# First attention's heads, the state space taps' layout and the phase corrections, reordered in one tuned kernel

## The chip, the cores and the metric

The kernel runs on one core of a Trainium2 chip. The metric is the device time of one execution in microseconds (us); the median of three runs is 1253.97 us (1253.89 to 1257.54). A core has five engines with a queue of their own each: PE (TensorE; its weight loads are shown as PEld), DVE (VectorE), ACT (ScalarE), POOL (GpSimd) and SP (SyncE), which issues most DMAs; ACT and POOL can issue DMAs too. An engine works its queue in order, and waits where an instruction's input isn't there or its output buffer isn't free.

## The reference

Two blocks and a feed-forward part over 512 tokens of 1024 columns, in float32. The change lies in the first block, which joins a state space mixer and sparse attention:

```python
ssm_u, ssm_z, q, k, v, attn_z, q_idx, k_idx, w_idx = jnp.split(h @ w_in[l], ...)
# s5_mixer: 32 groups of 16 channels, 64 complex states each
bu = jnp.einsum('gpc,bsgc->bsgp', b_bar, ug)
_, states = lax.associative_scan(_ssm_combine, (a_seq, bu), axis=1)
y = jnp.einsum('gcp,bsgp->bsgc', c_mat, states).real + d_skip * uf
z = jax.nn.gelu(y); z = z * jax.nn.sigmoid(z @ w_glu + b_glu)
# dsa_mixer: 8 heads of 64; an indexer of 8 heads picks 128 keys per query
q, k = rms_norm(q, q_gain), rms_norm(k, k_gain)
score = jnp.einsum('bqh,bqhs->bqs', wib, jax.nn.relu(rel))
_, sel = lax.top_k(score, topk)
logits = einsum(q, k[sel]) * scale + rel_bias[bucket(dist)]
```

The second block (a pooling mixer and attention over compressed, selected and window keys) and the feed-forward part are computed as before in both kernels.

## The kernel before, in words

**Order of work.** The program text is a set of generators. `weave(main, fill)` takes a step of the main stream, which asks for some time, and then steps of the filling stream (the projections, in 128x128 products) until that time is used. For PE and SP the order of the text is the order of the queue. For ACT, DVE and POOL a scheduler orders the instructions when the kernel is built, by readiness and by the memory that a step needs. Memory comes from a ring of 49 pages of 128x512 (`pg`, `pages`), and from named pools: the pool "ssm" (`self.sp`) holds the state space tiles, and its `ssmp.__exit__` releases that memory, which the pool "att1" (`self.att`) then takes. So what is written into "att1" waits for the last reader of the state space tiles.

**Products.** A product with a weight is made of three (L153 to L155): each weight chunk `wraw` is split into `whi` (a cast on ACT, L145) and `wlo` (a subtraction on DVE, L146). `proj` makes the queries and keys: a chain of 24 products into a PSUM buffer, then on ACT the copy `qk` (L658) and the square `sq` (L660), then a sum on DVE (L661).

**Index scores and mask.** `index_scores` makes, for three blocks of 256, 384 and 512 columns and 8 heads, a score in one of two PSUM buffers `ps_s` (L941, L942), a `relu` of it into a page on ACT (L944) and a weighted sum on DVE (L948). `top_mask` then runs 16 rounds of a maximum (L964) and a replacement (L965) on each block on DVE.

**State space part.** `ssm_tables` doubles a table of phases, n = 1, 2, 4 to 32, on POOL, and corrects the length of the last phase ahead of each doubling (L1204 to L1210). `ssm_taps` makes `We` and the taps `KK`; `ssm_scan` copies `E` out of PSUM on ACT (L1277), rotates it on POOL (L1281 to L1286), scans on DVE (L1288), rotates back (L1289 to L1294), and ends with `ssm_back` (the tiles `F`, L1228 to L1233) and the tile `TO`: a memset on POOL (L1298) and eight DMAs on ACT's queue (L1300), each a shifted part of `KK`. `bias_flip` transposes the attention's biases (L930) and copies them (`BT`, L931). `ssm_out` then makes for each group two products with a slice of `TO` as weights and four with `F` (L1314, L1318):

```python
nc.tensor.matmul(o[b], lhsT=self.TO[:, :, :, 2 * a + b], rhs=self.U(2 * a + b), start=True, stop=False)
```

A weight element there stands 32 elements behind the one before it. The result goes out on a DMA and comes back as `zi`; a gelu makes `zg` (L1330).

**First attention.** `norms` makes the reciprocal norms `rs`; then "ssm" is released. `attend` runs the heads: `early` of a head multiplies queries and keys by their norms on POOL (`qn` L716, `kn` L720; `qn` for a pair of heads), `prepare` transposes `kn` on PE (L734), splits it into the key stack (L148, L149) and makes the masks `bm` on POOL (L744, L745), and `prepare2` transposes `qn` (L727) and makes the query stacks (L888, L889). The steps of a head are the scores (L341, L342), the row maximum (L343, on DVE), the exponential (L345, ACT), the scaling by `rsum` (L350) and the transposes and products (L369, L383). DVE also works off products for a gate (`wadag`, L898).

Of the kernel before, what the change touches and what calls it, by code (L numbers as in the profile page):

```python
# [12 lines left out]
OP = mybir.AluOpType  # L13
# [48 lines left out]
def layout(inputs):  # L62
# [20 lines left out]
    skip = np.zeros((128, 16, 32), f)  # L83
    skip[112 + np.arange(16), np.arange(16)] = a["d_skip"][0].reshape(32, 16).T
# [20 lines left out]
class Kern:  # L105
# [342 lines left out]
    def block1(self):  # L448
# [238 lines left out]
        z = self.pages("zg", 4)  # L687
# [7 lines left out]
        ssmp.__exit__(None, None, None)  # L695
        attp = self.tc.tile_pool(name="att1", bufs=1)
        self.att = self.grp = attp.__enter__()
        self.qbufs = 4
# [10 lines left out]
        def head(h):  # L709
            hp = h // 2  # L710

            def early():
                if h % 2 == 0:
                    qns[h] = self.att.tile([128, 4, 128], F32, name="qn", tag="qn", bufs=1)
# [3 lines left out]
                kns[h] = self.att.tile([128, 4, 2, 64], F32, name="kn", tag="kn", bufs=1)  # L718
# [4 lines left out]
            def prepare2():  # L723
                if h % 2 == 0:
# [3 lines left out]
                    for hh in range(2):  # L728
                        qsts[h + hh] = self.q_stack(pq, hh, gq[:, 0:1])

            def prepare():
# [3 lines left out]
                kst = [self.att.tile([128, S], F32R, name="kst" + x, tag="kst" + x, bufs=2) for x in "hl"]  # L735
                self.split(pk, kst[0], kst[1], scale=gq[:, 1:2])
                bm = []
                for i in range(4):
                    w = (i + 1) * 128
                    b = self.att.tile([128, w], F32, name=f"bm{i}", tag=f"bm{i}", bufs=1)  # L740
# [56 lines left out]
        self.weave(self.attend([head(h) for h in range(8)], more=1.4), fill)  # L797
# [75 lines left out]
    def q_stack(self, pq, hh, gain):  # L873
        st = self.grp.tile([128, S], F32R, name="qst", tag="qst", bufs=self.qbufs)
        self.stack(st, pq, hh, gain)
        return st
# [200 lines left out]
    def ssm_loads(self):  # L1077
# [4 lines left out]
        self.skip = w[2].rearrange("p (c g) -> p c g", c=16)  # L1082
# [17 lines left out]
    def ssm_tables(self):  # L1100
# [101 lines left out]
        while n < 64:  # L1202

            g = [v[:, :, n - 1] for v in self.turn]  # L1204
            PTT(out=t1, in0=g[0], in1=g[0], op=OP.mult)
            PTT(out=t2, in0=g[1], in1=g[1], op=OP.mult)
            PTT(out=t1, in0=t1, in1=t2, op=OP.add)
            nc.gpsimd.tensor_scalar(t1, t1, -0.5, 1.5, op0=OP.mult, op1=OP.add)
            for v in g:
                PTT(out=v, in0=v, in1=t1, op=OP.mult)  # L1210
# [25 lines left out]
    def ssm_taps(self):  # L1236
# [16 lines left out]
        KK = self.pg("KK").rearrange("p (c g) -> p c g", c=16)  # L1253
        TT(out=KK, in0=kk.rearrange("p (g c) -> p c g", c=16), in1=self.skip, op=OP.add)
        self.KK = KK

    def ssm_scan(self):
# [41 lines left out]
        for r in range(8):  # L1299
            nc.scalar.dma_start(self.TO[0:128 - r * 16, 7 - r], self.KK[r * 16:128])  # L1300

# [558 lines left out]
```

## Time and profile before

| | before |
|---|---|
| median of 3 runs | 1253.97 us (1253.89 to 1257.54) |
| the profiled execution | 1254.35 us |
| its span in the trace | 1252.6 us |
| mean granted clock of PE | 0.974 |
| busy: PE, DVE, ACT, POOL | 92%, 65%, 44%, 37% |

Times of the trace count from the start of the span. A busy time is the time in which an engine has an instruction under way; "idle before" is the time that an engine stood still ahead of an instruction, and the name behind it is the work that ended that wait. Products overlap, so a product's own duration is longer than its share of the time; the distance from one start to the next, its pace, is what counts.

### The profile page before, as it was taken

What the parts mean: (1) busy time and instruction counts of PE and PEld (TensorE: products, weight loads), DVE (VectorE), ACT (ScalarE), POOL (GpSimd) and SP (SyncE); (2) the same over time, 40 slices, a digit from 0 to 9 for tenths busy, and PEclk for the clock granted to TensorE, in tenths of its full rate; (3) what the DMA queues carried; (4) which work ended last, traced back from release to release, by engine and by line L of the source; (5) the groups of instructions that cost most, each with busy time, mean ns of one, the idle gap of its engine ahead of it and who ended that gap; (6) DMA issues with size and microseconds to landing.
All of it is one profiled execution on the core that took longest, in us unless ns stands there. A gap on an engine that the chain in (4) does not pass through costs nothing.

```text
span 1252.6 us, 17118 instructions
## 1 busy us (share of the span) xinstructions
PE 1155.1 (92%) x6264; PEld 944.8 (75%) x6264; DVE 817.1 (65%) x1587; ACT 552.4 (44%) x1038; POOL 459.2 (37%) x546
## 2 busy tenths in 40 slices
PE   2786986977899999989999999999999999999998
PEld 2576886955678999877777677788888888888876
DVE  6888999257755476895667566554677743677731
ACT  4434522065644543556565556333544421344420
POOL 3859998068522135355756565201000000000000
PEclk9887988988999999999999999999999999999999
DMA  9452132163134533222111111134333223333330
GB/s 356 143 154 68 35 93 64 35 201 119 34 121 152 157 107 95 80 73 62 40 34 35 34 35 34 52 121 132 101 101 101 83 91 97 107 94 86 102 108 34
DMA packets 112756, 118.05 MB, mean 94 GB/s; under 512 B 16185, under 2 KB 101217, under 8 KB 112673
## 3 DMA queue, kind: packets, MB, share of 16 engines
q1 hardware_dynamic: 102432, 107.20, 27.2%
q10 hardware_dynamic: 10240, 9.77, 2.4%
q8 instruction: 49, 0.80, 0.3%
q14 instruction: 35, 0.28, 0.1%
HBM read 109.47 MB, written 6.30 MB: 92 GB/s over the span
## 4 chain that ended last, share of the span: by engine, by line
PE 78%; DVE 12%; issue 3%; ACT 2%; POOL 2%; DMA 1%; ACTq 0%; SPq 0%; POOLq 0%; DVEq 0%
PE ps_g L153 21%; PE ps_g L155 20%; PE ps_g L154 20%; PE ps_t L369 4%; PE ps_o L383 4%; DVE wlo L146 2%; PE ps_s L342 2%; PE ps_s L341 2%; DVE wada L490 1%; PE ps_t L1314 1%; DVE rb L1577 1%; PE ps_o L1652 1%; DVE t L1059 1%; PE ps_t L1318 1%; POOL P L350 1%
## 5 line engine op out<-in xcount | busy, mean ns | idle before, releaser
L145 ACT CAST whi<-wraw 128x1024 fp32r<-128x1024 f32 (+4 forms) x161 | 161.8, 1012 | 168.9 <-PE ps_g L154 146.6
L146 DVE TENSOR_TENSOR wlo<-wraw,whi 128x1024 fp32r<-128x1024 f32 (+4 forms) x143 | 176.4, 1239 | 60.1 <-ACT whi L145 59.7
L153 PE MATMUL ps_g<-hT,whi 128*128 128x512 f32 x504 | 206.8, 410 | 0.0
L155 PE MATMUL ps_g<-hT,wlo 128*128 128x512 f32 x504 | 197.8, 392 | 0.0
L154 PE MATMUL ps_g<-hT,whi 128*128 128x512 f32 x504 | 196.4, 390 | 0.0
L350 POOL TENSOR_TENSOR P<-P,rsum 128x256 f32<-128x256 f32 (+3 forms) x144 | 100.5, 727 | 77.1 <-DVE rsum L1439 29.7
L345 ACT ACTIVATE P<-P,nm 128x128 f32<-128x128 f32 (+3 forms) x160 | 89.6, 560 | 84.0 <-DVE nm L343 82.7
L153 PEld LDWEIGHTS ps_g<-hT,whi 128*128 128x128 f32 x504 | 95.2, 189 | 24.5 <-issue 9.3
L155 PEld LDWEIGHTS ps_g<-hT,wlo 128*128 128x128 f32 x504 | 94.7, 188 | 22.0
L154 PEld LDWEIGHTS ps_g<-hT,whi 128*128 128x128 f32 x504 | 95.1, 189 | 18.1 <-issue 1.2
L343 DVE CUSTOM_DVE_ANT_0 P<-ps_s,att 128x128 f32<-128x128 f32 (+3 forms) x128 | 62.1, 485 | 50.5 <-PE ps_t L369 27.1
L369 PE MATMUL ps_t<-consts,P 128*128 128x128 f32 x400 | 67.4, 284 | 12.3 <-DVE qst L889 7.2
L153 PE MATMUL ps_g<-whi,hTh 128*128 128x256 f32 x192 | 59.8, 311 | 12.1 <-ACT whi L145 6.6
L153 PE MATMUL ps_g<-act,whi 128*128 128x512 f32 (+1 forms) x176 | 70.7, 402 | 0.0
L155 PE MATMUL ps_g<-act,wlo 128*128 128x512 f32 (+1 forms) x176 | 69.1, 393 | 0.0
L154 PE MATMUL ps_g<-act,whi 128*128 128x512 f32 (+1 forms) x176 | 68.5, 389 | 0.0
L369 PEld LDWEIGHTS ps_t<-consts,P 128*128 128x128 f32 x400 | 47.6, 143 | 27.4 <-issue 15.0
L849 POOL TENSOR_TENSOR acc<-acc,sq 128x512 f32<-128x512 f32 x15 | 22.0, 1464 | 117.6 <-ACT sq L848 115.0
L153 PE MATMUL ps_g<-whi,hT 128*128 128x256 f32 (+1 forms) x216 | 61.0, 282 | 1.4 <-ACT sq L1354 1.3
L154 PE MATMUL ps_g<-wlo,hT 128*128 128x256 f32 (+1 forms) x216 | 60.5, 280 | 0.0
L155 PE MATMUL ps_g<-whi,hT 128*128 128x256 f32 (+1 forms) x216 | 60.5, 280 | 0.0
L154 PE MATMUL ps_g<-wlo,hTh 128*128 128x256 f32 x192 | 55.3, 288 | 5.5 <-DVE wlo L146 5.5
(509 smaller groups left out, 2902.5 us busy)
## 6 DMA issues: line engine op xcount, KB each, us to landing
wraw<-in_w_in_dram SPq DMA_DIRECT2D x56, 512.0 KB, 3.6
wraw<-in_w_up_dram SPq DMA_DIRECT2D x40, 512.0 KB, 3.7
wada<-in_w_ada_dram SPq DMA_DIRECT2D x16, 512.0 KB, 7.3
wraw<-in_w_down_dram SPq DMA_DIRECT2D x16, 512.0 KB, 3.4
wadag<-in_w_ada_dram SPq DMA_DIRECT2D x8, 512.0 KB, 4.6
wraw<-in_w_out_dram SPq DMA_DIRECT2D x8, 512.0 KB, 3.4
wraw<-in_w_attn_br_dram SPq DMA_DIRECT2D x8, 512.0 KB, 3.4
wraw<-in_w_o_dram SPq DMA_DIRECT2D x8, 512.0 KB, 3.5
```

The lines of the kernel that those rows point to most:

```text
L145: nc.scalar.copy(hi, src)
L146: (eng or nc.vector).tensor_tensor(out=lo, in0=src, in1=hi, op=OP.subtract)
L153: mm(out, lhsT=l[0], rhs=r[0], start=start, stop=False)
L154: mm(out, lhsT=l[0], rhs=r[1], start=False, stop=False)
L155: mm(out, lhsT=l[1], rhs=r[0], start=False, stop=stop)
L341: nc.tensor.matmul(s, lhsT=q, rhs=khi[:, :w], start=True, stop=False)
L342: nc.tensor.matmul(s, lhsT=q, rhs=klo[:, :w], start=False, stop=True)
L343: nc.vector.tensor_tensor_reduce(out=P[i], in0=s, in1=madd(i), scale=-1.0, scalar=3.0e38, op0=OP.add, op1=OP.min, accum_out=nm[:, i:i + 1])
L345: nc.scalar.activation(P[i], P[i], AF.Exp, scale=-1.0, bias=nm[:, i:i + 1], accum_out=sums[:, i:i + 1])
L350: nc.gpsimd.tensor_tensor(out=P[n], in0=P[n], in1=sc[:, n:n + 1].to_broadcast([128, (n + 1) * 128]), op=OP.mult)
L369: nc.tensor.transpose(pt[:, o:o + 128], P[i][:, j * 128:(j + 1) * 128], self.ident)
L383: nc.tensor.matmul(acc[x * 64:(x + 1) * 64, j * 128:], lhsT=V(j), rhs=tiles[b][:, o:o + w], start=start and j == 0, stop=stop and j == 2)
```

## The change

1. **Taps.** The host's `skip` and the tile `KK` are laid out (group, channel) and no longer (channel, group), and `TO` with them. Behind the eight DMAs, eight new copies on ACT write `TOg`, eight pages with the 128x128 weights of four groups each, and `ssm_out` reads these.
2. **Phase corrections** are made for n = 1 and 8 only, no longer for all six n.
3. **Heads.** `early` of heads 0 to 2 and `prepare` and `prepare2` of head 0 are called before `ssmp.__exit__`; their tiles, of heads 0 to 2 and of head 0, are pages of the ring. The four `zg` pages are taken at the end of `ssm_out`.

```diff
...
     c = [pairs(a[n]).transpose(1, 3, 0, 2).reshape(128, 256) for n in ("c_re", "c_im")]
-    skip = np.zeros((128, 16, 32), f)
-    skip[112 + np.arange(16), np.arange(16)] = a["d_skip"][0].reshape(32, 16).T
+    skip = np.zeros((128, 32, 16), f)
+    skip[112 + np.arange(16), :, np.arange(16)] = a["d_skip"][0].reshape(32, 16).T
     row = lambda w: np.tile(w.reshape(1, -1), (128, 1))
...
-        z = self.pages("zg", 4)
+        z = []
         fill = self.both(proj(1024, qf), proj(1536, kf), self.gemm_tn(hT, 8, w_in, 2048, 512, ev_v),
...
         norms()
-        ssmp.__exit__(None, None, None)
-        attp = self.tc.tile_pool(name="att1", bufs=1)
-        self.att = self.grp = attp.__enter__()
-        self.qbufs = 4
         self.pool_scale = (0, 1)
...
                 if h % 2 == 0:
-                    qns[h] = self.att.tile([128, 4, 128], F32, name="qn", tag="qn", bufs=1)
+                    qns[h] = self.room("qn", 512, h <= 2).rearrange("p (t d) -> p t d", t=4)
                     for t in range(4):
...
                             in1=rs[0].rearrange("p (t h) -> p t h", t=4)[:, t, hp * 2:hp * 2 + 2, None].to_broadcast([128, 2, 64]), op=OP.mult)
-                kns[h] = self.att.tile([128, 4, 2, 64], F32, name="kn", tag="kn", bufs=1)
+                kns[h] = self.room("kn", 512, h <= 2).rearrange("p (t a d) -> p t a d", t=4, a=2)
                 for t in range(4):
...
                     for hh in range(2):
-                        qsts[h + hh] = self.q_stack(pq, hh, gq[:, 0:1])
+                        qsts[h + hh] = self.q_stack(pq, hh, gq[:, 0:1], h == 0)
...
                     nc.tensor.transpose(pk[:, t * 128:(t + 1) * 128], kns[h][:, t].rearrange("p h d -> p (h d)"), self.ident)
-                kst = [self.att.tile([128, S], F32R, name="kst" + x, tag="kst" + x, bufs=2) for x in "hl"]
+                kst = [self.pg("kst", F32R) if h == 0 else self.att.tile([128, S], F32R, name="kst" + x, tag="kst" + x, bufs=2) for x in "hl"]
                 self.split(pk, kst[0], kst[1], scale=gq[:, 1:2])
...
                     w = (i + 1) * 128
-                    b = self.att.tile([128, w], F32, name=f"bm{i}", tag=f"bm{i}", bufs=1)
+                    b = self.room(f"bm{i}", w, h == 0)
                     m = sel[i]
...
                          self.gemm_nt(zT, 4, self.cols(A["w_glu"], 0, 512), ev_glu))
-        self.weave(self.attend([head(h) for h in range(8)], more=1.4), fill)
+        heads = [head(h) for h in range(8)]
+        for h in range(3):
+            heads[h].pop("early")()
+        first = heads[0].pop("prepare")()
+        heads[0].pop("prepare2")()
+        heads[0]["prepare"] = lambda: first
+        ssmp.__exit__(None, None, None)
+        attp = self.tc.tile_pool(name="att1", bufs=1)
+        self.att = self.grp = attp.__enter__()
+        self.qbufs = 4
+        self.weave(self.attend(heads, more=1.4), fill)
         self.dump("y", y[0])
...
-    def q_stack(self, pq, hh, gain):
-        st = self.grp.tile([128, S], F32R, name="qst", tag="qst", bufs=self.qbufs)
+    def room(self, name, n, page):
+
+        return self.pg(name)[:, :n] if page else self.att.tile([128, n], F32, name=name, tag=name, bufs=1)
+
+    def q_stack(self, pq, hh, gain, page=False):
+        st = self.pg("qst", F32R) if page else self.grp.tile([128, S], F32R, name="qst", tag="qst", bufs=self.qbufs)
         self.stack(st, pq, hh, gain)
...
         self.Bm, self.CT = ([v[:, x * 256:(x + 1) * 256].rearrange("p (a c) -> p a c", c=16) for x in range(2)] for v in w[:2])
-        self.skip = w[2].rearrange("p (c g) -> p c g", c=16)
+        self.skip = w[2].rearrange("p (g c) -> p g c", c=16)
         self.rb = self.load("rel_bias", self.sp)
...
         while n < 64:
-
-            g = [v[:, :, n - 1] for v in self.turn]
-            PTT(out=t1, in0=g[0], in1=g[0], op=OP.mult)
-            PTT(out=t2, in0=g[1], in1=g[1], op=OP.mult)
-            PTT(out=t1, in0=t1, in1=t2, op=OP.add)
-            nc.gpsimd.tensor_scalar(t1, t1, -0.5, 1.5, op0=OP.mult, op1=OP.add)
-            for v in g:
-                PTT(out=v, in0=v, in1=t1, op=OP.mult)
+            if n in (1, 8):
+
+                g = [v[:, :, n - 1] for v in self.turn]
+                PTT(out=t1, in0=g[0], in1=g[0], op=OP.mult)
+                PTT(out=t2, in0=g[1], in1=g[1], op=OP.mult)
+                PTT(out=t1, in0=t1, in1=t2, op=OP.add)
+                nc.gpsimd.tensor_scalar(t1, t1, -0.5, 1.5, op0=OP.mult, op1=OP.add)
+                for v in g:
+                    PTT(out=v, in0=v, in1=t1, op=OP.mult)
             f = [v[:, :, n - 1:n].to_broadcast([128, 16, n]) for v in self.turn]
...
             yield 1.0
-        KK = self.pg("KK").rearrange("p (c g) -> p c g", c=16)
-        TT(out=KK, in0=kk.rearrange("p (g c) -> p c g", c=16), in1=self.skip, op=OP.add)
+        KK = self.pg("KK").rearrange("p (g c) -> p g c", c=16)
+        TT(out=KK, in0=kk.rearrange("p (g c) -> p g c", c=16), in1=self.skip, op=OP.add)
         self.KK = KK
...
         self.ssm_back()
-        self.TO = self.sp.tile([128, 8, 16, 32], F32, name="TO", tag="TO", bufs=1)
-        nc.gpsimd.memset(self.TO.rearrange("p a b c -> p (a b c)"), 0.0)
+        TO = self.sp.tile([128, 8, 32, 16], F32, name="TO", tag="TO", bufs=1)
+        nc.gpsimd.memset(TO.rearrange("p a b c -> p (a b c)"), 0.0)
         for r in range(8):
-            nc.scalar.dma_start(self.TO[0:128 - r * 16, 7 - r], self.KK[r * 16:128])
+            nc.scalar.dma_start(TO[0:128 - r * 16, 7 - r], self.KK[r * 16:128])
+        W = self.pages("TOg", 8)
+        for i in range(8):
+            nc.scalar.copy(W[i].rearrange("p (g r c) -> p g r c", g=4, c=16), TO[:, :, 4 * i:4 * i + 4].rearrange("p r g c -> p g r c"))
+        self.taps = lambda g: W[g // 4][:, g % 4 * 128:(g % 4 + 1) * 128]
...
                 for b in range(2):
-                    nc.tensor.matmul(o[b], lhsT=self.TO[:, :, :, 2 * a + b], rhs=self.U(2 * a + b), start=True, stop=False)
+                    nc.tensor.matmul(o[b], lhsT=self.taps(2 * a + b), rhs=self.U(2 * a + b), start=True, stop=False)
                 for x in range(2):
...
         yield 0.0
+        z.extend(self.pages("zg", 4))
         for n in range(4):
...
```

The queues of PE and SP keep their order, with `TOg` in the place of `TO`. Three places of the others follow.

ACT, near the index scores of the last block, before (names: `relu` of the scores, `E` the state input, `qk` and `sq` the query and key gemms):

```order
L944 ACTIVATE relu<-ps_s 128x512
L1277 COPY E<-ps_t 128x512
L944 ACTIVATE relu<-ps_s 128x512 x3
L658 COPY qk<-ps_g 128x256
L660 ACTIVATE sq_1503<-ps_g 128x256
L944 ACTIVATE relu<-ps_s 128x512 x2
L658 COPY qk<-ps_g 128x256
L660 ACTIVATE sq_1551<-ps_g 128x256
```

ACT, further down, before: the DMAs of `TO`, then the copies `BT` of the biases and the value `V`:

```order
L660 ACTIVATE sq_1968<-ps_g 128x256
L145 CAST whi<-wraw 128x1024
L1300 DMA TO<-KK 128x512
L1300 DMA TO<-KK 112x512
L1300 DMA TO<-KK 96x512
L1300 DMA TO<-KK 80x512
L1300 DMA TO<-KK 64x512
L1300 DMA TO<-KK 48x512
L1300 DMA TO<-KK 32x512
L1300 DMA TO<-KK 16x512
L931 COPY BT<-ps_t 128x512 x2
L671 COPY V<-ps_g 128x256
```

ACT in the change, behind the second of the pairs `qk` and `sq` that stand among these relu:

```order
L658 COPY qk<-ps_g 128x256
L660 ACTIVATE sq_1491<-ps_g 128x256
L1311 DMA TO<-KK 128x512
L1311 DMA TO<-KK 112x512
L1311 DMA TO<-KK 96x512
L1311 DMA TO<-KK 80x512
L1311 DMA TO<-KK 64x512
L1311 DMA TO<-KK 48x512
L1311 DMA TO<-KK 32x512
L1311 DMA TO<-KK 16x512
L1314 COPY TOg<-TO 128x512 x8
L954 ACTIVATE relu<-ps_s 128x512 x4
```

The DMAs of `TO` and the new copies now stand ahead of the last four relu, and of the eleven pairs `qk` and `sq` and the casts that follow them.

POOL, at the start of the attention, before (`Fi` the last state space tile, `qn` and `kn` the normed queries and keys, `bm` the masks of a head, here of head 0):

```order
L1233 TENSOR_TENSOR Fi_1441<-t_1442,t_1443 128x512
L716 TENSOR_TENSOR qn<-qk,rs 128x128 x4
L720 TENSOR_TENSOR kn<-qk,rs 128x128 x4
L745 TENSOR_TENSOR bm_2514<-consts,BT 128x128
L745 TENSOR_TENSOR bm_2516<-score_569,BT 128x256
L744 TENSOR_TENSOR bm_2518<-score_570,far_bias 128x128
L745 TENSOR_TENSOR bm_2518<-score_570,BT 128x256
L744 TENSOR_TENSOR bm_2521<-score_571,far_bias 128x256
L745 TENSOR_TENSOR bm_2521<-score_571,BT 128x256
L720 TENSOR_TENSOR kn<-qk,rs 128x128 x4
L716 TENSOR_TENSOR qn<-qk,rs 128x128 x4
L720 TENSOR_TENSOR kn<-qk,rs 128x128 x4
```

POOL in the change, same place; `bm_2548` to `bm_2555` are head 1's masks, in the pool "att1", and the first `kn` is head 3's:

```order
L1244 TENSOR_TENSOR Fi_1413<-t_1414,t_1415 128x512
L741 TENSOR_TENSOR bm_2548<-consts,BT 128x128
L741 TENSOR_TENSOR bm_2550<-score_569,BT 128x256
L740 TENSOR_TENSOR bm_2552<-score_570,far_bias 128x128
L741 TENSOR_TENSOR bm_2552<-score_570,BT 128x256
L740 TENSOR_TENSOR bm_2555<-score_571,far_bias 128x256
L741 TENSOR_TENSOR bm_2555<-score_571,BT 128x256
L716 TENSOR_TENSOR kn<-qk,rs 128x128 x4
L712 TENSOR_TENSOR qn<-qk,rs 128x128 x8
L716 TENSOR_TENSOR kn<-qk,rs 128x128 x8
L712 TENSOR_TENSOR qn<-qk,rs 128x128 x4
L716 TENSOR_TENSOR kn<-qk,rs 128x128 x4
```

The norms of heads 0 to 2 stand behind head 1's masks, and head 0's own masks come after the last row shown.

DVE, at the first row maxima (L343) of head 0, before (`wadag` the gate's products, `gate` the reading of their sums):

```order
L146 TENSOR_TENSOR wlo<-wraw,whi 128x1024 x2
L898 ISA wadag,gate<-wadag,cB 128x1024
L898 ISA gate 128x1
L898 ISA wadag,gate<-wadag,cB 128x1024
L898 ISA gate 128x1
L343 ISA P_2594,nm<-ps_s,bm_2514 128x128
L343 ISA nm 128x1
L898 ISA wadag,gate<-wadag,cB 128x1024
L898 ISA gate 128x1
L343 ISA P_2595,nm<-ps_s,bm_2516 128x256
```

DVE in the change (L908 and L899 are L898 and L889 of before):

```order
L908 ISA wadag,gate<-wadag,cB 128x1024
L908 ISA gate 128x1
L908 ISA wadag,gate<-wadag,cB 128x1024
L908 ISA gate 128x1
L899 SCALAR_TENSOR_TENSOR qst<-ps_t,gq,qst 64x512
L908 ISA wadag,gate<-wadag,cB 128x1024
L908 ISA gate 128x1
L149 SCALAR_TENSOR_TENSOR kstl<-ps_t,gq,ksth 128x512
L685 SCALAR_TENSOR_TENSOR ga<-ga,ps_g 128x512
L908 ISA wadag,gate<-wadag,cB 128x1024
L908 ISA gate 128x1
L343 ISA P_2586,nm<-ps_s,bm_2502 128x128
```

Another `wadag` product stands a few rows ahead of these, so five now precede the first maximum, where two did.

## Rows read from the trace of the kernel before

**Rows 1.** The page's busy time: engine, us, share of the span, instructions.
```profile
PE 1155.1 (92%) x6264; PEld 944.8 (75%) x6264; DVE 817.1 (65%) x1587; ACT 552.4 (44%) x1038; POOL 459.2 (37%) x546
```

**Rows 2.** Windows of 50 us: window, length, busy us of PE, PEld, DVE, ACT, POOL, clock, DMA.
```profile
150.00:200.00 50.00, 34.85 (x273) 33.50 (x272) 49.69 (x92) 13.95 (x31) 49.69 (x31) 0.86 0.34 98
```

**Rows 3.** Timeline of ACT: start us, duration us, operation, [idle before and releaser].
```profile
134.76 0.59 ACT L1277 COPY E<-ps_t 128x512 f32<-128x512 f32 x1 [0.49 <-PE ps_t L1274]
...
145.49 1.08 ACT L944 ACTIVATE relu<-ps_s 128x512 f32<-128x512 f32 x2 [2.79 <-DVE score L948]
...
190.40 8.64 ACTq L1300 DMA_DIRECT2D TO<-KK  x8
199.08 1.07 ACT L931 COPY BT<-ps_t 128x512 f32<-128x512 f32 x2 [9.61 <-DMA TO<-KK]
```

**Rows 4.** Timeline of PE.
```profile
146.13 0.50 PE L941 MATMUL ps_s<-kk,iq 128*128 128x512 f32 x1 [1.98 <-ACT relu L944]
...
146.82 0.28 PE L154 MATMUL ps_g<-wlo,hTh 128*128 128x256 f32 x1
146.94 0.28 PE L155 MATMUL ps_g<-whi,hTl 128*128 128x256 f32 x1
...
185.81 1.02 PE L930 MATMUL ps_t<-btf,consts 128*128 128x512 f32 x2
...
199.72 2.08 PE L930 MATMUL ps_t<-btf,consts 128*128 128x512 f32 x2 [9.61 <-ACT BT L931]
...
205.46 0.98 PE L1314 MATMUL ps_t<-U,TO 128*128 128x64 f32 x4
```

**Rows 5.** Timeline of POOL.
```profile
139.63 1.29 POOL L1281 TENSOR_TENSOR rot<-turn,E 128x512 f32<-128x512 f32 x1
...
184.64 2.27 POOL L1294 TENSOR_TENSOR Sti<-rot 128x512 f32<-128x512 f32 x1
186.84 3.52 POOL L1298 MEMSET TO<- 128x4096 f32 x1
```

**Rows 6.** Groups by line, POOL, 100 to 216 us: count, busy us, mean ns.
```profile
L1210 POOL TENSOR_TENSOR turn<-turn,kt 128x16 f32<-128x16 f32 x10 | 2.8, 300 | 0.4
...
L1207 POOL TENSOR_TENSOR kt<-kt,kt 128x16 f32<-128x16 f32 x5 | 2.3, 463 | 0.4
...
L1205 POOL TENSOR_TENSOR kt<-turn 128x16 f32<-128x16 f32 x5 | 1.6, 316 | 0.0
...
L1208 POOL TENSOR_SCALAR kt<-kt 128x16 f32<-128x16 f32 x5 | 1.4, 284 | 0.4
L1206 POOL TENSOR_TENSOR kt<-turn 128x16 f32<-128x16 f32 x5 | 1.3, 265 | 0.4
```

**Rows 7.** The view of the tile TO: durations min, median, max; landing.
```profile
L1300 ACTq DMA_DIRECT2D TO<-KK x8: 532/607/620, 190.4 to 198.5; - x8
...
DMA to landing us min/median/max: 1.9/3.4/5.9
```

**Rows 8.** Groups by line and form, 130 to 262 us.
```profile
L1314 PEld LDWEIGHTS ps_t<-U,TO 128*128 128x128 f32 x64 | 15.3, 307 | 0.1
...
L1330 ACT ACTIVATE zg<-zi 128x512 f32<-128x512 f32 x3 | 3.3, 1156 | 0.0
```

**Rows 9.** Windows of 10 us.
```profile
160.00:170.00 10.00, 6.04 (x54) 5.85 (x52) 9.96 (x15) 1.68 (x4) 10.00 (x7) 0.97 0.17 53
170.00:180.00 10.00, 8.42 (x54) 8.42 (x55) 9.97 (x23) 4.99 (x12) 10.00 (x8) 0.69 0.56 159
```

**Rows 10.** Timelines at the attention's start: POOL, ACT, PE, DVE.
```profile
251.68 1.47 POOL L716 TENSOR_TENSOR qn<-qk,rs 128x128 f32<-128x128 f32 x4 [36.73 <-PE ps_t L1318]
...
264.24 1.98 ACT L145 CAST whi<-wraw 128x1024 fp32r<-128x1024 f32 x2
...
269.74 0.31 PE L341 MATMUL ps_s<-ksth,qst 128*128 128x128 f32 x1
...
272.30 0.29 DVE L343 CUSTOM_DVE_ANT_0 P<-ps_s,bm 128x128 f32<-128x128 f32 x1
```

## The prediction, made before the changed kernel was run

> **What bounds the kernel now.** First the page's busy time: PE works 92% of the span [rows 1], so whatever moves PE's work moves the end. The change touches the stretch from 100 to 290 us. In the windows of 50 us PE is busy 34.85 of 50 between 150 and 200 us, and DVE and POOL 49.69 each [rows 2]: there the vector engines set the pace. After 300 us PE has the same instructions in the same order in both kernels and little idle time, so I carry a shift of the attention's start to the end one to one. This one stretch decides.
>
> The timeline of ACT [rows 3] shows how an engine's queue orders that stretch. The index scores' relu of heads 4 and 5 runs at 145.49. Much later, at 190.40, the eight DMAs that build the tile TO are issued on ACT's queue, and the next BT copy stands 9.61 us idle until 199.08, released by DMA TO<-KK: what is queued on ACT behind these DMAs waits for them. The timeline of PE [rows 4] has the other half. At 146.13 PE's score product for head 6 waits for the relu (1.98 us): the scores have two PSUM buffers, so PE goes nowhere until that relu has run. Behind it come 270 gemm products at a pace of 0.12 us, then the BT transposes from 185.81, a wait of 9.61 us until 199.72, and the first product with TO at 205.46.
>
> **Contiguous taps: what moves on ACT.** Eight copies TOg are added behind the TO DMAs. In the order of ACT the DMAs and copies now stand ahead of the relu of heads 4 to 7, ahead of eleven pairs qk and sq of the key and query gemms, and ahead of the whi casts between them. Before, all of these came first. PE's order is unchanged. So PE must stand from about 144 us until the DMAs and copies are done. That time is the sum of three terms.
>
> *POOL's memset of TO.* It ends at 186.84 + 3.52 = 190.36, and POOL runs up to it almost without a gap [rows 2, 5]. The corrections for n of 2 to 32 take 2.8 + 2.3 + 1.6 + 1.4 + 1.3 = 9.4 us [rows 6]; four of these five go: 7.5 us. They lie on POOL's own chain into the scans. The first rotation followed the tables at once, at 139.63 [rows 5]; its second E page was copied by 135.35 [rows 3], so at least 139.63 + 1.29 - 135.35 = 5.5 us can be won, and E covers little beyond 7.5. I take the whole 7.5: the memset ends at 182.9. Later ends: 190.4 if DVE's scans hold POOL where they were; earlier: 178, since with DVE's work cut down in the stall an operation like the 2.27 us one at 184.64 may take the 1.29 of the one at 139.63 [rows 5].
>
> *The DMAs.* Eight issues of 0.607 us, the median, are 4.9 us, and the last lands 3.4 us later, the median [rows 7]: 8.3 us. Low end 4.9 + 1.9 = 6.8, high end the 8.64 us that the issues took before [rows 3] and 5.9, 14.5.
>
> *The copies.* The trace has no copy that gathers 16-element runs out of TO. Nearest below are the BT copies of the same 128x512, 1.07 us for two [rows 3], 0.54 each; nearest above the gelu into zg, which reads with a stride, 1.156 us [rows 8]. I take 0.54, as the runs are whole: 8 x 0.54 = 4.3 us, high end 9.2. The Trainium skill (SBUF — State Buffer, section Door 1: The DMA port swizzle) says that full rate needs repeated hits in a 16-byte line; runs of 16 floats fulfil that, a stride of one float per line would not. By it 4.3, against it 9.2.
>
> So the relu of head 4 runs at R = 182.9 + 8.3 + 4.3 = 195.5 instead of 145.49. SP's order is the same, and its loads run ahead until their buffers are full. Nothing hides these 50 us: PE waits for ACT, DVE finishes the top-mask rounds of the block of 384 columns and then waits for the scores.
>
> **From the relu to the first product with TO.** Before: 205.46 - 145.49 = 60.0, of which the 9.61 us wait for BT goes, because the DMAs that caused it are already done: 50.4. Of the 39.7 us from 146.13 to 185.81 the 270 gemms need 270 x 0.12 = 32.4 and the two pairs of score products about 1; some 6 us are waits and slow clock [rows 4]. The stall lets DVE finish the rounds that caused part of these waits, so I take 46, with ends 44.4 and 50.4. The first product with TO comes at 195.5 + 46 = 241.5. After PE's idle time in 160 to 170 us the granted clock in 170 to 180 was 0.69 [rows 9]. The Trainium skill (TensorE: Matmul & The Clock Gate, section What's actually happening) has an idle array fall to 1.2 GHz and regain 2.4 GHz under load. A stall of 50 us meets that case, and by it alone the saving that I take would be lost again: the sum would stay at the end 50.4.
>
> **Inside ssm_out.** From 205.46 to the release of the last state product at 251.68 [rows 10] are 46.2 us. The 64 weight loads of TO, strided, hold 15.3 us, 307 ns each [rows 8]; at the gemms' pace of 0.12, whose loads are contiguous, they would take 7.7. So 7.6 us go, the only gain on PE's path: 38.6 us. The end E is 241.5 + 38.6 = 280.1 instead of 251.7: **28.4 us later**.
>
> **Fewer corrections** otherwise only shorten a POOL queue that then waits; counted above. The host's and KK's new layout adds no instruction and costs nothing.
>
> **Heads in pages ahead of the release.** The text of the program puts head 0's norms and masks before the pool's release, but in POOL's order the six masks of head 1, in the new pool's memory, now stand first behind the last Fi, then kn of head 3, then qn and kn of the first heads, then head 0's masks. POOL stood idle 36.73 us until 251.68, released by the last state product [rows 10]; it will stand idle again, and the norms in pages with it. Head 0's kn then comes behind six masks and twelve norm operations instead of four norms: four take 1.47 us [rows 10], so eight more are 2.9, and six masks at the same price 2.2: about 5 us later. Against that the zg and whi operations precede the key stacks on ACT: the casts at 264.24 come nearer to E, and the first score product, at 269.74, or 18 us after E, by about 2. On DVE five gate products precede the first row maximum, which stood at 272.30 behind two. These cancel: I take 0, with 6 us either way, somewhat more than that delay.
>
> Sum: the profiled run took 1254.35 us, 0.4 above the median of 1253.97. 1254.35 + 28.4 = 1282.8; I forecast **1283**.
>
> **Rivals.** *A shorter stall (1269).* The memset ends at 178 (4.9), the fill takes 44.4 (1.6), the attention's start gains 6, the DMAs 1.5: 14 less, 1269. For it: POOL's short operations [rows 5]; against it: E and DVE's scans still feed POOL. 0.18.
>
> *A longer stall (1297).* DVE keeps the memset at 190.4 (7.5 more) and copies cost 1.156 (4.9 more), with half of the 4.4 of the clock: 14.6 more, 1297. For it: DVE was as full as POOL [rows 2]. 0.17.
>
> *Faster (1237).* The relu don't wait, because the memset is done early, and ACT reaches them in time. Then TO's loads (7.6) and the BT wait (9.6) are gained: 1254.35 - 17.2 = 1237. It decides at the R for which E stays at 251.7: R = 251.7 - 38.6 - 46 = 167.1, a memset that ends at 154.5. For it: ACT was idle most of 150 to 200 (13.95 us busy [rows 2]) and could do the work early. Against it: the scans that precede the memset on POOL can't start before 134 or so, and took 47 us. 0.05.
>
> *The heads do run ahead.* If the norms and masks in pages came before the release, despite the order, the start would gain those 5 us and the 2.9 that qn and kn took from 251.68 on: 1275, inside the range. 0.03. A stall that just balances its gains: 0.02.
>
> **The numbers.** The forecast has 0.55. The range of 1265 to 1298 takes in the short and the long stall, and leaves out the faster and balanced cases and the sum of all the high ends. A measurement here tells 0.3% (4 us) from no change: faster 0.06, same 0.02, slower 0.92.
>
> **What would show it.** In the changed profile: PE idle some 50 us before the score product of head 6, released by ACT's relu; relu behind eight TOg copies of about 0.54 us, those behind DMA TO; the memset ending near 183; PE busy well below 20 in the window 150 to 200; no wait for BT; the TO loads near 0.12 us; POOL idle until the last state product and then head 1's masks first. The forecast falls if the relu run before the TO DMAs on the chip, if the memset ends before 165, or if the attention's start moves by more than 6 us against E.

## The result and the profile after

The changed kernel takes **1289.22 us** (1288.54 to 1290.66, four executions), the kernel before, measured beside it, 1254.55 us (1253.89 to 1257.54, four): a ratio of 1.0273 [1.0254, 1.0292], 34.7 us slower. The profiled execution took 1289.2 us, with a span of 1287.4.

The page's busy times show PE with the same work in a longer span (92% before [rows 1]):

```profile
PE 1151.1 (89%) x6264; PEld 940.2 (73%) x6264; DVE 819.7 (64%) x1587; ACT 557.2 (43%) x1046; POOL 438.0 (34%) x522
```

The windows of 50 us of the changed kernel (columns: PE, PEld, DVE, ACT, POOL busy with their instructions, PE's granted clock, DMA share, GB/s):

```profile
150.00:200.00 50.00, 4.69 (x18) 4.31 (x19) 37.41 (x73) 6.43 (x12) 45.84 (x35) 0.50 0.08 24
200.00:250.00 50.00, 50.00 (x425) 47.41 (x425) 37.91 (x82) 19.30 (x40) 7.95 (x7) 0.99 0.25 75
250.00:300.00 50.00, 38.31 (x278) 33.31 (x278) 13.97 (x10) 15.09 (x21) 16.88 (x40) 0.89 0.32 97
```

Between 150 and 200 us PE works 4.69 of 50 us where it worked 34.85 [rows 2]. Two views say why. The timeline of ACT (start, duration, instruction, idle time before it and its releaser):

```profile
146.54 0.39 ACT L660 ACTIVATE sq<-ps_g 128x256 f32<-128x256 f32 x1
...
183.86 5.11 ACTq L1311 DMA_DIRECT2D TO<-KK  x8
190.51 4.25 ACT L1314 COPY TOg<-TO 128x512 f32<-128x512 f32 x8 [43.57 <-DMA TO<-KK]
194.67 1.07 ACT L954 ACTIVATE relu<-ps_s 128x512 f32<-128x512 f32 x2
```

and that of PE:

```profile
195.31 0.80 PE L951 MATMUL ps_s<-kk,iq 128*128 128x512 f32 x1 [48.73 <-ACT relu L954]
...
237.30 0.55 PE L1329 MATMUL ps_t<-U,TOg 128*128 128x64 f32 x4
...
285.23 1.55 PE L730 MATMUL ps_t<-consts,kn 128*128 128x128 f32 x4 [4.79 <-POOL kn L716]
...
298.10 1.09 PE L730 MATMUL ps_t<-consts,kn 128*128 128x128 f32 x4 [6.89 <-DVE kst L149]
...
303.56 0.22 PE L341 MATMUL ps_s<-kst,qst 128*128 128x128 f32 x1
...
317.90 0.33 PE L369 MATMUL ps_t<-consts,P 128*128 128x128 f32 x1 [1.32 <-POOL P L350]
```

From 146.93 to 190.51 ACT runs nothing: the DMAs are issued only at 183.86, right behind the memset, which ends at 183.82, and the copies wait until they have landed. The relu of heads 4 and 5, whose scores were done at 145.89, stand behind both; before, this relu ran at 145.49 [rows 3]. PE, whose next score product needs the relu's buffer, stands 48.73 us. The weight loads of the taps then cost less (by shape, with total busy time and mean ns; 307 ns before [rows 8]):

```profile
L1329 PEld LDWEIGHTS ps_t<-U,TOg 128*128 128x128 f32 x64 | 8.6, 190 | 0.2
```

At the attention's start PE waits for the key norms `kn` and for the key stack `kst`, 4.79 and 6.89 us. Before, its waits there were 4.79 us for a cast `whi` and 2.43 for a key stack:

```profile
265.32 0.80 PE L153 MATMUL ps_g<-hTh,whi 128*128 128x512 f32 x1 [4.79 <-ACT whi L145]
...
279.76 0.63 PE L734 MATMUL ps_t<-consts,kn 128*128 128x128 f32 x4 [2.43 <-DVE kstl L149]
```

In the changed kernel again, on POOL, the memset of TO, and the first and the last operation of its chain of masks and norms at the attention's start:

```profile
180.31 3.51 POOL L1309 MEMSET TO<- 128x4096 f32 x1
...
277.05 0.46 POOL L741 TENSOR_TENSOR bm<-consts,BT 128x128 f32<-128x128 f32 x1 [68.78 <-PE ps_t L1333]
...
293.21 0.72 POOL L741 TENSOR_TENSOR bm<-score,BT 128x256 f32<-128x256 f32 x1
```

On DVE, the splits of two weight chunks beside that chain, the first of them 8.03 us long by itself, and the first row maximum:

```profile
286.98 9.16 DVE L146 TENSOR_TENSOR wlo<-wraw,whi 128x1024 fp32r<-128x1024 f32 x2 [6.03 <-ACT whi L145]
...
306.38 0.29 DVE L343 CUSTOM_DVE_ANT_0 P<-ps_s,bm 128x128 f32<-128x128 f32 x1
```

The shift can be read at four places (us from the span's start). The time at which the last state product releases POOL is the prediction's E; the first residual sum is DVE's first addition into the residual (L816 before, L822 now):

| | before | after | shift |
|---|---|---|---|
| score product of head 6 | 146.13 | 195.31 | +49.2 |
| E | 251.7 | 277.05 | +25.4 |
| first transpose of probabilities, L369 | 287.49 | 317.90 | +30.4 |
| first residual sum | 377.0 | 411.4 | +34.4 |

The stall costs 49.2; of these 24 come back by E; then 9 more are lost at the attention's start. After that the shift stays to the end.

### The profile page after: what moved, and what is told of

Same layout as the page of the kernel before. It is cut to its first block, busy times and chain, and to the rows that moved or that the text cites. A ratio compares the mean times of both kernels' runs of the same rounds, so it can differ in the third digit from the quotient of the medians.

```text
span 1287.4 us, 17101 instructions
## 1 busy us (share of the span) xinstructions
PE 1151.1 (89%) x6264; PEld 940.2 (73%) x6264; DVE 819.7 (64%) x1587; ACT 557.2 (43%) x1046; POOL 438.0 (34%) x522
## 4 chain that ended last, share of the span: by engine, by line
PE 76%; DVE 11%; POOL 5%; issue 4%; ACT 2%; DMA 1%; ACTq 1%; SPq 0%; DVEq 0%; POOLq 0%
PE ps_g L153 20%; PE ps_g L154 20%; PE ps_g L155 20%; PE ps_t L369 4%; PE ps_o L383 4%; PE ps_s L342 2%; PE ps_s L341 2%; POOL tw L1069 1%; DVE wlo L146 1%; DVE wada L490 1%; DVE rb L1593 1%; PE ps_o L1668 1%; POOL t L1069 1%; PE ps_t L1333 1%; DVE score L975 1%
## 5 line engine op out<-in xcount | busy, mean ns | idle before, releaser
L146 DVE TENSOR_TENSOR wlo<-wraw,whi 128x1024 fp32r<-128x1024 f32 (+4 forms) x143 | 180.2, 1265 | 78.6 <-ACT whi L145 78.4
L343 DVE CUSTOM_DVE_ANT_0 P<-ps_s,att 128x128 f32<-128x128 f32 (+3 forms) x128 | 62.1, 485 | 50.9 <-PE ps_t L369 25.9
L369 PE MATMUL ps_t<-consts,P 128*128 128x128 f32 x400 | 68.3, 285 | 13.2 <-DVE qst L899 7.1
L369 PEld LDWEIGHTS ps_t<-consts,P 128*128 128x128 f32 x400 | 48.0, 144 | 29.0 <-issue 14.6
```

What stands on the lines that cost most here:

```text
L146: (eng or nc.vector).tensor_tensor(out=lo, in0=src, in1=hi, op=OP.subtract)
L343: nc.vector.tensor_tensor_reduce(out=P[i], in0=s, in1=madd(i), scale=-1.0, scalar=3.0e38, op0=OP.add, op1=OP.min, accum_out=nm[:, i:i + 1])
L369: nc.tensor.transpose(pt[:, o:o + 128], P[i][:, j * 128:(j + 1) * 128], self.ident)
```

## The experiments

My theory before them: TO's DMAs, placed on ACT's queue ahead of the relu, hold them (all of the loss up to E), and the heads part loses the rest at the attention's start. Rivals: the copies, the layout or the missing corrections themselves cost time, or the heads part costs nothing.

**1. The DMAs and copies written behind the bias flip.** Everything else as in the change.

```diff
-  ... self.hold(22.0), self.bias_flip(), self.ssm_out(z)
+  ... self.hold(22.0), self.bias_flip(), self.ssm_lay(), self.ssm_out(z)
+        self.TO = TO
+
+    def ssm_lay(self):
+        nc, TO = self.nc, self.TO
         for r in range(8):
...
+        yield 0.0
```

> The changed kernel with one thing moved: the eight DMAs of TO and the eight copies TOg are written behind the bias flip, directly ahead of ssm_out, so on ACT's queue they stand behind all relu of the index scores and all qk and sq. Theory (the 48.7 us in which PE waits for the relu of head 4 come from the DMAs and copies that stand ahead of it on ACT): that wait falls under 3 us, ssm_out ends near 243 to 248 us instead of 276.8, the attention's start stays as late against it as in the changed kernel, and the time is 1250 to 1260 us. Rival (the wait comes from the ring of pages, which the eight TOg pages make short, wherever the copies stand): the wait stays above 25 us and the time above 1275 us.

1255.63 us (1254.45 to 1259.46), ratio 1.000 [0.9987, 1.0013]. Of the wait of 48.73 us 5.06 are left, more than the 3 that I allowed (experiment 4 returns to that), and the whole loss is gone:

```profile
150.65 0.79 PE L951 MATMUL ps_s<-kk,iq 128*128 128x512 f32 x1 [5.06 <-ACT relu L954]
...
202.20 0.71 PE L1334 MATMUL ps_t<-U,TOg 128*128 128x64 f32 x4 [4.82 <-ACT TOg L1318]
```

The copies themselves now cost PE one wait of 4.82 us, in the place of the 9.61 for BT [rows 4]. So the stall comes from the place in ACT's queue, and neither from the copies nor from the layout. That the time just equals the one before is a balance: E comes at 247.06, 4.6 us earlier than before, and the attention's start, with the first L369 41.3 us behind E as in the change (35.8 before), takes that back.

**2. The heads part undone.** The change with `early`, `prepare` and `prepare2` back behind the release, and no pages for their tiles. The `zg` pages stay at the end of `ssm_out`, in this and in all later kernels.

```diff
+        ssmp.__exit__(None, None, None)
+        attp = self.tc.tile_pool(name="att1", bufs=1)
...
-        for h in range(3):
-            heads[h].pop("early")()
-        first = heads[0].pop("prepare")()
...
```

> The changed kernel with its third part undone: norms, masks and stacks of the first heads are again in the pool att1 and written behind the release. Theory (the first heads lose about 9.5 us because POOL does head 1's masks and twelve norms ahead of head 0's kn, and DVE's wlo split of 8 us stands beside POOL's work): the stall on ACT stays, the kn transposes stand 3 to 4 us behind the end of ssm_out again, and the time is 1278 to 1282 us. Rival (the start is late because the stall shifted it against the weight loads and the clock): the time stays at 1286 to 1290 us.

1281.79 us (1279.80 to 1282.69), ratio 1.0200 [1.0183, 1.0218]: the stall stays (49.2 us), and 7.4 us of the loss go. The first L369 comes at 313.6, 37.1 behind E at 276.47; in the change it is 40.9 behind. So the heads part doesn't gain: it costs 7 us, or 9 by the two ratios (beside this run the kernel before took 1256.15 us).

**3. The taps undone.** Heads part and fewer corrections alone, with `TO` and its DMAs as before.

```diff
-        W = self.pages("TOg", 8)
...
+        self.taps = lambda g: TO[:, :, :, g]
```

> The changed kernel with its first part undone: strided TO, no copies, the old layout. Theory (the copies and DMAs ahead of the relu are the stall): no wait of PE for a relu above 3 us, TO's weight loads at 307 ns again, the memset some 6 us earlier than before the change, the attention's start late by 5 to 9 us; 1255 to 1264 us. Rival (the four phase corrections that went, or the head pages, moved the DMAs ahead): the stall stays and the time is above 1280 us.

1260.96 us, ratio 1.0041 [1.0025, 1.0056]: no stall, and a loss of 5 us. Not all of it is the heads part's: E comes at 254.16, 2.5 us later than before, though no head has begun by then, and from E to the first residual sum it is 128.3 us, 3.0 more than before. Two things missed: the memset of TO was to start 6 us earlier for want of four corrections, and it started at 186.6, as before; and PE still waits 4.56 us for a relu, where I had allowed 3.

**4. The corrections alone.** The kernel before with `if n in (1, 8)` (and the later `zg` pages).

> The kernel before with the second part alone: phase corrections for n of 1 and 8. Theory (they lie on POOL's chain to the memset of TO, and the DMAs behind it held the BT copies 9.6 us): the memset ends 5 to 8 us earlier, the wait for BT falls to about 3 us, and the time is 1246 to 1251 us. Rival (DVE's splits set the pace there anyway): 1253 to 1256 us.

1258.26 us (ten executions), ratio 1.0012 [1.0001, 1.0023]: nothing is gained. The theory fails; the rival's mechanism holds, but the time is above its range too. The windows of 10 us of this kernel, where POOL and DVE were both full before [rows 9]:

```profile
160.00:170.00 10.00, 10.00 (x91) 10.00 (x90) 9.97 (x20) 3.55 (x7) 6.90 (x5) 1.00 0.01 3
170.00:180.00 10.00, 7.98 (x56) 7.78 (x56) 10.00 (x17) 2.92 (x8) 7.99 (x5) 0.83 0.45 121
```

DVE stays full, and POOL now waits, first for ACT, whose relu and `E` copies stand in one queue, then for DVE's scans:

```profile
136.61 1.28 POOL L1286 TENSOR_TENSOR rot<-turn,E 128x512 f32<-128x512 f32 x1 [4.25 <-ACT relu L948]
...
164.16 1.30 POOL L1295 TENSOR_TENSOR rot<-turn,E 128x512 f32<-128x512 f32 x1 [1.16 <-DVE E L1293]
...
172.01 2.16 POOL L1294 TENSOR_TENSOR rot<-turn,E 128x512 f32<-128x512 f32 x1 [3.95 <-DVE E L1293]
...
186.90 3.53 POOL L1303 MEMSET TO<- 128x4096 f32 x1
```

So DVE sets most of the pace there, and time taken off POOL comes back as waiting. Fewer corrections even seem to cost some 2 us, at the edge of what these times can tell: E comes at 254.06, where it came at 251.68, and PE waits 5.08 us for the relu ahead of head 6, where it waited 1.98 [rows 4]. That wait is 4.56 to 5.06 in the other kernels with two corrections and no stall (experiments 1, 3, 6 and 9), and 1.95 in experiments 7 and 8, which keep all six. Why is not shown.

**5. All six corrections in the changed kernel.**

```diff
-            if n in (1, 8):
+            if True:
```

> The changed kernel with all six phase corrections. By the prediction's step the memset of TO would end 7.5 us later, at 191, and the time be near 1296 us. Theory after e4 (with the corrections gone POOL only waits for E and for DVE's scans instead): the memset ends 1 to 5 us later than in the changed kernel, and the time is 1289 to 1294 us.

1288.44 us (1287.46 to 1289.83), ratio 1.0269 [1.0255, 1.0283], below the theory's range of 1289 to 1294. The memset was to end 1 to 5 us later than in the change; it starts at 180.5, as there:

```profile
180.47 3.51 POOL L1309 MEMSET TO<- 128x4096 f32 x1
```

So the corrections were not why it comes 6.5 us earlier there than before. What remains is the stall: the memset starts at 180.1 to 180.5 in the three kernels that have it (the change, experiments 2 and 5), and at 186.5 to 187.7 in all others. It keeps DVE's other work away (37.41 us busy from 150 to 200, against 49.69 [rows 2]), and POOL's operations of 128x512, up to 2.27 us before [rows 5], take 1.10 to 1.31 each in it from 157 us to the memset. That the second follows from the first is the likely reading; no run takes DVE's work away by itself.

**6. POOL's order at the attention's start mended.** On top of experiment 1: the norms of heads 1 and 2 and everything of `attend` issued behind the last mask of head 0.

```diff
+        ready = self.masked
...
+        with self.tc.issue_after(ready.ins):
+            for h in range(1, 3):
+                heads[h].pop("early")()
...
-        self.weave(self.attend(heads, more=1.4), fill)
+        self.weave(behind(self.attend(heads, more=1.4)), fill)
```

> The kernel of e1 with POOL's order mended: head 0's norms and masks are tied ahead of every other norm and mask of the heads, so nothing that waits for the pool's release stands before them on POOL. Theory (the first heads are late because head 0's kn queue behind head 1's masks, and because DVE's wlo split of 8 us stands beside POOL's run of norms): head 0's qn, kn and masks run before the end of ssm_out, PE's wait of 4.8 us for kn goes, the wlo split falls below 4 us, and the time is 1245 to 1251 us. Rival (the gate products that DVE does ahead of head 0's row maximum, eight of them here, set the start): the waits move to the row maxima and the time stays at 1253 to 1258 us.

1257.65 us, ratio 1.0023 [1.0009, 1.0038]. Head 0's norms do run ahead, and the splits on DVE are short again, but nothing is won. POOL and DVE of this kernel:

```profile
230.94 1.47 POOL L712 TENSOR_TENSOR qn<-qk,rs 128x128 f32<-128x128 f32 x4 [16.18 <-issue]
236.04 1.47 POOL L716 TENSOR_TENSOR kn<-qk,rs 128x128 f32<-128x128 f32 x4 [3.63 <-issue]
246.32 0.45 POOL L741 TENSOR_TENSOR bm<-consts,BT 128x128 f32<-128x128 f32 x1 [8.80 <-PE ps_t L1346]
...
256.75 2.77 POOL L712 TENSOR_TENSOR qn<-qk,rs 128x128 f32<-128x128 f32 x2
```

```profile
256.56 1.31 DVE L146 TENSOR_TENSOR wlo<-wraw,whi 128x1024 fp32r<-128x1024 f32 x1 [5.69 <-ACT whi L145]
258.05 1.23 DVE L146 TENSOR_TENSOR wlo<-wraw,whi 128x1024 fp32r<-128x1024 f32 x1 [0.17 <-ACT whi L145]
...
276.87 1.23 DVE L146 TENSOR_TENSOR wlo<-wraw,whi 128x1024 fp32r<-128x1024 f32 x1 [1.17 <-ACT whi L145]
278.01 0.28 DVE L343 CUSTOM_DVE_ANT_0 P<-ps_s,bm 128x128 f32<-128x128 f32 x1
```

Head 0's masks still wait until 246.32, for the last products with `TOg` (L1346), and between 259.19 and 274.17 DVE works off eight gate products (L920, 1.23 us each, with waits for their DMAs) ahead of head 0's first row maximum at 278.01. PE waits 7.40 us for `kst` and 5.95 for `kstl`. My theory failed here; the rival's time and its late row maximum came true. That the gate products alone hold the start is not shown by this run: experiment 9 moves them, and wins nothing.

**7. Contiguous taps alone, at the later place.** The kernel before with the new layout and `ssm_lay` of experiment 1, six corrections, no heads part.

> The kernel before with contiguous taps alone, their DMAs and copies behind the bias flip: all six corrections, heads as before. Theory (the taps are worth the 6.7 us of weight loads, less the wait for the copies, and the heads' part costs 5 us or more): ssm_out ends 4 to 6 us earlier than in the kernel before, no wlo split above 2.5 us at the attention's start, and the time is 1247 to 1251 us, 0.3 to 0.6% below the kernel before. Rival (what ssm_out gains, the wait for the copies or the attention's start takes back): 1253 to 1257 us.

**1249.59 us** (1247.74 to 1250.85), ratio 0.9957 [0.9944, 0.9969], faster than both kernels by these intervals. E comes at 245.21, 6.5 earlier than before. The waits of PE between 100 and 300 us (in all, times, longest):

```profile
PE ps_t L1328 <- ACT TOg L1312: 6.0, 1, 6.0
...
PE ps_t L934 <- ACT BT L935: 0.8, 1, 0.8
```

The wait of 9.61 for BT became one of 6.0 for the first copy.

**8. The same, each copy right ahead of its first use.**

```diff
+        def taps(g):
+            if g // 4 not in W:
...
+                nc.scalar.copy(W[i].rearrange("p (g r c) -> p g r c", g=4, c=16), TO[:, :, 4 * i:4 * i + 4].rearrange("p r g c -> p g r c"))
+            return W[g // 4][:, g % 4 * 128:(g % 4 + 1) * 128]
```

> Contiguous taps alone (six corrections, no heads in pages), the eight DMAs behind the bias flip, and each of the eight TOg copies written right ahead of the first product that reads it, not all eight at once. Theory: in the version with all eight copies at once PE's waits inside the output part were 6.0 us for the first TOg and one of 6.6 us for a whi cast, which stood behind the copies on ACT; with one copy at a time the whi cast no longer queues behind eight copies, some 2 to 4 us are won: 1246 to 1248. Rival: the first TOg wait, set by the memset and the DMAs, decides, and the rest is absorbed: 1249 to 1251. Second rival: ACT now makes PE wait at some of the later seven copies, which come behind other work of ACT: 1252 or more.

**1246.47 us** (1245.64 to 1250.11), ratio 0.9938 [0.992, 0.9956], the best version. The time is the theory's, its mechanism isn't: PE waits 4.7 us for a whi cast in both versions, and the wait of 6.6 stands at 99.7 us in the version of experiment 7, long before the copies. What differs is the first copy, at 200.86 against 201.95, and PE's wait for a key stack at the attention's start, 2.66 us against 3.73, and the intervals of the two ratios overlap. Whether one copy at a time is worth anything by itself stays open.

**9. The heads part once more, its gate products moved.** Experiment 8 with two corrections and the heads part of experiment 6, and the gate's sums one projection later.

```diff
...
-        fill = self.both(fill, self.gate_sums(), self.gemm_nt(hT, 8, self.cols(w_in, 512, 256), ev_gs), z_split(),
+        fill = self.both(fill, self.gemm_nt(hT, 8, self.cols(w_in, 512, 256), ev_gs), self.gate_sums(), z_split(),
...
```

> The same taps with copies one at a time, two corrections, the heads part with POOL's order mended (head 0's norms and masks ahead of the last state product, those of heads 1 and 2 behind them), and the gate's products one projection later in the filling stream, so that they no longer stand on DVE ahead of head 0's first row maximum. Theory: the eight gate products (1.23 us each) were what held the first row maximum at 278.0 us when POOL's order alone was mended; without them the first product of probabilities and values comes 3 to 7 us sooner than the 281.7 us of the version without the heads part, and the time is 1241 to 1247. Rival: head 0's masks, whose last waits for the last state product's buffer, and the casts of the weights on ACT hold the start where it was: 1248 to 1252. Second rival: the gate products only move, and hold later row maxima: 1250 to 1256.

1260.62 us, ratio 1.0041 [1.0025, 1.0057]: a clear miss, above the theory and both rivals' ranges. The gate products only moved to between 267.6 and 288 (the second rival's mechanism), and the long split is back. POOL and DVE of this kernel:

```profile
253.61 2.91 POOL L716 TENSOR_TENSOR kn<-qk,rs 128x128 f32<-128x128 f32 x8
...
259.32 1.48 POOL L712 TENSOR_TENSOR qn<-qk,rs 128x128 f32<-128x128 f32 x4
```

```profile
254.78 8.25 DVE L146 TENSOR_TENSOR wlo<-wraw,whi 128x1024 fp32r<-128x1024 f32 x2 [5.55 <-ACT whi L145]
262.95 0.74 DVE L149 SCALAR_TENSOR_TENSOR kst<-ps_t,gq,kst 128x512 fp32r<-128x512 f32 x1
```

`kst` stands on DVE behind that split, and PE waits 11.53 us for it.

## Why the prediction was right, and where not

The forecast of 1283 with a range of 1265 to 1298 holds the 1289.22. Step by step:

| step | predicted | in the changed kernel's trace |
|---|---|---|
| memset of TO ends | 182.9 | 180.31 + 3.51 = 183.8 |
| its DMAs: end of memset to first copy | 8.3 | 190.51 - 183.8 = 6.7 |
| eight copies | 4.3 | 4.25 |
| relu of head 4 (R) | 195.5 | 194.67 |
| relu to first TO product | 46 (44.4 to 50.4) | 237.30 - 194.67 = 42.6 |
| first TO product | 241.5 | 237.30 |
| weight loads with TO saved | 7.6 | 15.3 - 8.6 = 6.7 |
| first TO product to E | 38.6 | 277.05 - 237.30 = 39.8 |
| E | 280.1 | 277.05 |
| attention's start against E | 0, 6 either way | +9.0 up to the first residual sum |

**The stall was right**, in cause, place and size: ACT's in-order queue, the two score buffers, about 50 us. Experiment 1 shows the cause, since moving the DMAs and copies alone brings the time back to 1255.63.

**The memset's term had about the right size by luck.** I took the 7.5 us of four corrections off POOL's chain. Experiments 3 to 5 show them to be worth nothing there: in experiment 4 the first rotation comes at 136.61, 3.0 us earlier and not the 5.5 or more that I read, the scans take that back, and the memset starts when it did. The 6.5 us came from the stall itself. The text had this as the earlier end, "with DVE's work cut down in the stall", and it was the whole of the effect.

**The stretch behind the stall was shorter than its low end**, 42.6 against 44.4. I let some of the waits and of the slow clock of the stretch before stay. The longest of these waits, which neither my rows nor my sum named, was

```profile
171.58 0.58 PE L153 MATMUL ps_g<-whi,hTh 128*128 128x256 f32 x1 [5.54 <-ACT sq L660]
```

and it is gone. The granted clock was 0.50 in the stall; in the changed kernel's windows behind it

```profile
195.00:199.00 4.00, 3.69 (x13) 3.31 (x14) 3.50 (x3) 1.64 (x4) 3.86 (x3) 0.50 0.00 0
199.00:203.00 4.00, 4.00 (x31) 4.00 (x31) 3.83 (x4) 0.96 (x3) 3.91 (x3) 0.81 0.00 0
203.00:207.00 4.00, 4.00 (x37) 4.00 (x37) 3.86 (x11) 1.94 (x4) 3.76 (x5) 1.00 0.00 0
207.00:237.00 30.00, 30.00 (x244) 28.08 (x243) 29.00 (x69) 13.55 (x30) 1.27 (x1) 1.00 0.42 124
```

it was back at 1.00 from 203 us on, and the windows show PE busy without a gap from 199 to 237. The clock behaved as the Trainium skill (TensorE: Matmul & The Clock Gate, section What's actually happening) has it, half speed (1.2 GHz) when idle and full under load, but the cost that I let it stand for, the end of 50.4, did not come.

**The step that failed is "These cancel: I take 0".** Of the attention's start the parts were right: head 1's masks stood first on POOL, POOL stood idle 68.78 us until the last state product, head 0's `kn` came later, by 6 us against E where I had 5 (the six masks took 3.4 us, not 2.2), and the wait of 4.79 us for a cast went. But the terms never cancelled by my own rows: 5 us later against 2 earlier leaves 3, and I gave the three further gate products on DVE no price, though one takes 1.2 us. And I left out that two engines can block each other: the split of the nearer weight chunk comes onto DVE while POOL's chain still runs, takes 8.03 us where two took 2.36 before, and `kst`, which stands behind it, comes 6.89 us late on PE.

The result is beyond the 6 us that I named as a sign of being wrong. Head 0's first score product stands 26.5 us behind E (18.1 before), its first row maximum 29.3 (20.6), the first residual sum 134.4 (125.3); only at the first L369 is it 5.0 more. Experiment 2 prices the heads part, in the stall, at 7 to 9 us.

What within the heads part costs this stays in part open. The collision is not all of it: in experiment 6 the splits are short, and the first score product stands 19.6 us behind the start of the last state products (18.6 before, 27.2 in the change), yet the first row maximum stands 31.6 behind it (21.2 before, 30.0 in the change). There the gate products stand between the two; no run has both them and the long split out of the way with the heads part in place. The further 3 to 4 us between the first L369 and the first residual sum (93.5 us against 89.5 before; 90.0 in experiment 2) were not tracked down either.

**In the sum** two misses worked against each other: E came 3 us earlier than forecast, the start 9 later, and the forecast was 6 us short.

Of the rivals the shorter stall had the right sign up to E (25.4 us later, between its 20.4 and my 28.4), but not for the start, from which it expected a gain. The faster case would have needed a memset that ends at 154.5; the same saving, got by moving the DMAs back instead, was there in experiments 7 and 8: 5.3 and 8.5 us of the 17.2 named.

## What to carry to other kernels

A DMA that waits in a compute engine's queue can hold all that is queued behind it, here for 43.57 us: put it behind the work that doesn't need its result, above all where another engine stands on a two-buffer handshake with that work. Before taking time off an engine, look which engine is full beside it: with POOL and DVE both at 100%, relieving POOL gave nothing. Work that is moved "ahead" can land beside a DVE operation with two SBUF inputs, so look what DVE does for PE while a row of small operations runs on POOL. And price every operation that moves in front of the first one on the critical path, also those that seem to cancel.

## What the runs showed that I had not expected

A split on DVE (two inputs in SBUF, 128x1024, 1.21 us alone) that came while POOL ran masks and norms back to back did not slow down in proportion: in five kernels it ended about one own duration after POOL's run ended.

| kernel | POOL's run ends | split starts | split takes | ends after POOL's end |
|---|---|---|---|---|
| changed | 293.93 | 286.98 | 8.03 | 1.08 |
| experiment 1 | 263.95 | 257.04 | 7.99 | 1.08 |
| experiment 3 | 271.05 | 264.32 | 7.80 | 1.07 |
| experiment 5 | 294.59 | 287.31 | 8.37 | 1.09 |
| experiment 9 | 260.80 | 254.78 | 7.11 | 1.09 |

In the kernel before and in experiments 2, 4, 7 and 8 POOL's run ends before the split starts, and it takes 1.2 us. The Trainium skill (SBUF — State Buffer, section Who interferes with whom) says that such a DVE instruction contends with GpSimd instructions that read SBUF, and that the one issued second blocks for the whole of the other. These rows agree on the blocking, and go further: it lasted for all of the 15 or 16 POOL operations of 0.40 to 0.74 us that were left, not for one.

It can also go the other way. In experiment 6 the split starts at 256.56, beside the same kind of run, and takes 1.31 us; there POOL's operations are the ones held, 1.37 to 1.46 us for a `qn` or `kn` that takes 0.39 otherwise (the first two are the 2.77 us above), one beside each of the two splits and of most gate products behind them. What decides which engine is held for long is not shown, and no run took POOL's operations alone away from beside the split.
